# Opening of a two-layer fp32 trunk on one core: norm weights and activation table first, the norm factor ahead of the first column-wise blocks, and hidden-state transposes in two batches of four

## The chip, the cores and the metric

The kernel runs on one core of one Trainium2 chip. The metric is the device time of one execution in microseconds. The kernel before took 961.47 us (median of three runs, 961.28 to 961.77). Below, PE is TensorE's matrix multiply, PEld its weight load, DVE is VectorE, ACT is ScalarE, POOL is GpSimd, SP is SyncE. The last two only do small work here; SP issues nearly all loads.

## What is computed

The input is 256 rows of 1024 floats. Two layers follow each other; each is a half-step SwiGLU feed-forward block, a mixer and a second half-step feed-forward block, each behind an RMS norm, and a last norm ends the trunk:

```python
def rms_norm(x, g):
    y = x * rsqrt(mean(x * x, axis=-1, keepdims=True) + EPS)
    return y * g

def swiglu(x, w_gate, w_up, w_down):
    return (silu(x @ w_gate) * (x @ w_up)) @ w_down

for layer in range(2):
    h = h + 0.5 * swiglu(rms_norm(h, ffn1_norm[layer]), ...)      # 1024 -> 2816 -> 1024
    h = h + mixer(rms_norm(h, mix_norm[layer]), ...)
    h = h + 0.5 * swiglu(rms_norm(h, ffn2_norm[layer]), ...)
return rms_norm(h, final_norm)
```

The change touches only the first feed-forward block of layer 0 (`ffn(0, begin)`), that is, the opening of the kernel. The mixers (dilated attention with spatial gating in layer 0, block attention in layer 1) are not touched.

## The kernel before

**Precision.** Every fp32 product is made from three matmuls of a rounded format: an operand is split into a high part (`hi`, a rounded copy made on ACT) and a low part (`lo`, the rest, made on DVE by a subtraction), and the three are high by high, high by low and low by high. Weights are split as they arrive: `split_parts` (L79 on ACT, L80 on DVE), in two halves of 128x1024 for each 1 MB weight tile (tiles 0 and 1 in four quarters).

**The stream of weights.** `Stream` numbers the weight tiles in the order of their use. Each is 1 MB. Three raw buffers (`RAW = 3`) and four split buffers (`SPL = 4`) rotate: the load of tile j starts when tile j-3 has been split, and its split may start when PE has finished with tile j-4. `add` (L46) sets in how many DMAs a tile is loaded: four for tiles 0 and 1, two for tiles 2 and 3, one for all others. Tiles 0 and 1 are the gate weights of the first 512 hidden columns, 2 and 3 the up weights of the same columns; from tile 4 on gate and up tiles of 256 hidden columns alternate (4 and 5 for the third pair of hidden tiles, 6 and 7 for `k = 6`, 8 and 9 for `k = 8`, up to `k = 20`).

**The opening (`begin`, L431 to L539).** The first input is loaded already transposed (`xf`, eight tiles of 128x256, with `fetch`), multiplied by the norm weights `gT` and split into `xgh` and `xgl` (`part`, L470 and L471). The norm's factor for each row is not yet known. PE first runs 28 warm-up matmuls on zeros (`heat`, L429), then the first 512 gate columns and the first 512 up columns row-wise (`products`, L459, L462, L465) on `xgh`/`xgl` of tiles 0 to 3. Two blocks of 256 hidden columns follow column-wise (`colwise`, L352 to L354, 48 matmuls of 256 columns each): m = 0 with weight tile 4 and m = 1 with weight tile 5, both still on `xgh`/`xgl`.

Meanwhile `x` arrives by rows, its squares are summed, and POOL makes the factor `rstd` (L212). The factor is spread over all partitions: `dg` (L514) puts it on a diagonal, four plain fp32 matmul records of ones by `dg` (L515) put it in a PSUM bank `rb`, and two copies on ACT (L518) put it twice side by side in `rs`. With `rs` the transposed input is normed in place on DVE (L522, eight tiles) and split again into `xT["h"]` on ACT (L205) and `xT["l"]` on DVE (L206), in four pairs of tiles. All later column-wise blocks read `xT`. In the code before this whole chain stands inside m = 1, behind the split of weight tile 5 and ahead of the second column-wise block.

**After the opening.** For k = 6, 8, ... 20 two column-wise blocks (gate and up, 96 matmuls in all) give two tiles of the hidden state, `gated` (L554, L555) multiplies them and `keep` splits them into `hT`. The four hidden tiles of the first 512 columns were computed row-wise and must be transposed: `finish` leaves a function `turn` for each half of the rows in the list `todo`; a `turn` is four plain fp32 transposes on PE (L567) and a split (L205, L206). At k = 8 `turn_all` runs all that is in the list, which is both functions here. In the other three feed-forward blocks one `turn` runs before k = 4 and the other at k = 8. The block ends with `project`, the product with the down weights (L369, L370, L373).

**What sets the order.** The tile framework's planner writes each engine's order. `begin`, the two `finish` and one `keep` stand under `tc.manual_schedule()`: on each engine these keep the order in which they are written. Work from behind that block (the splits of weight tiles 6 to 9, for instance) may be put between them where the planner sees the engine free. Every engine runs its own list strictly in that order.

Of the kernel before, what the change touches and what calls it, by code (L numbers as in the profile page):

```python
# [10 lines left out]
F32 = mybir.dt.float32  # L11
F32R = mybir.dt.float32r
AF = mybir.ActivationFunctionType
ALU = mybir.AluOpType

S = 256
D = 1024
NT = S // 128
KD = D // 128
# [17 lines left out]
class Stream:  # L37
# [5 lines left out]
        self.loaded = self.split = self.done = self.next = 0  # L43

    def add(self, src, nk, w, shift=0, pieces=2):
        self.specs.append((src, nk, w, (4, 4, 2, 2)[len(self.specs)] if len(self.specs) < 4 else 1, shift, pieces))  # L46

    def load_one(self):
        for _ in self.load_parts():
# [68 lines left out]
def trunk(ctx: ExitStack, tc: tile.TileContext, a, out):  # L118
    nc = tc.nc
# [11 lines left out]
    def bank():  # L131
        return ps.tile([128, 512], F32, name="bank")
# [48 lines left out]
    gT = cp.tile([128, 6 * KD], F32, name="gT")  # L181
    xr = [cp.tile([128, D], F32, name=f"x{t}") for t in range(NT)]

    half_neg = cp.tile([128, 8], F32, name="half_neg")
    ident = cp.tile([128, 128], F32, name="ident")
# [7 lines left out]
    ones = cp.tile([128, 128], F32, name="ones")  # L193
# [10 lines left out]
    def split(hi, lo, src):  # L204
        nc.scalar.activation(hi, src, AF.Copy)  # L205
        nc.vector.tensor_sub(lo, src, hi.bitcast(F32))  # L206


    xT = {}
# [4 lines left out]
    pend, rstd = {}, {}  # L214
# [119 lines left out]
    def new_xT():  # L334
        xT["h"] = xp.tile([128, KD, NT, 128], F32R, name="xTh")
        xT["l"] = xp.tile([128, KD, NT, 128], F32R, name="xTl")
# [9 lines left out]
    def colwise(p, w, c, x=None):  # L346

        for k in range(KD):
            cs = slice(c * 128, (c + 1) * 128)
            h, l = w[0][:, k, cs], w[1][:, k, cs]  # L350
            xh, xl = [v[:, k] for v in (x or (xT["h"], xT["l"]))]
            nc.tensor.matmul(p, h, xh, start=k == 0, stop=False)  # L352
            nc.tensor.matmul(p, h, xl, start=False, stop=False)  # L353
            nc.tensor.matmul(p, l, xh, start=False, stop=k == KD - 1)  # L354
# [71 lines left out]
    def heat(n):  # L426

        for _ in range(n):
            nc.tensor.matmul(bank()[:, :128], warm, warm, start=True, stop=True)  # L429

    def begin(fp, pb):  # L431

        f = [fp.tile([128, KD, S], t, name=m) for t, m in ((F32, "xf"), (F32R, "xgh"), (F32R, "xgl"))]
        xf, xgh, xgl = f

        def fetch(k, n, engine):
            engine.dma_start(xf[:, k : k + n, :], a["xt"][:, k : k + n, :])

        fetch(0, 1, nc.scalar)
        nc.scalar.dma_start(gT, a["gt"])  # L440
        first = st.load_parts()
        next(first)
        fetch(1, 1, nc.sync)
        next(first)
        fetch(2, 2, nc.sync)
        for _ in first:
            pass
        fetch(4, 2, nc.sync)
        second = st.load_parts()
        next(second)  # L450
        next(second)
        fetch(6, 2, nc.sync)
        for _ in second:
            pass
        st.load_one()

        def products(m, w, k0, k):
            for t in range(NT):
                nc.tensor.matmul(pb[t, m], xgh[:, k0 + k, t * 128 : (t + 1) * 128], w[0][:, k, :],  # L459
                                 start=k0 + k == 0, stop=False)  # L460
            for t in range(NT):
                nc.tensor.matmul(pb[t, m], xgl[:, k0 + k, t * 128 : (t + 1) * 128], w[0][:, k, :],  # L462
                                 start=False, stop=False)
            for t in range(NT):
                nc.tensor.matmul(pb[t, m], xgh[:, k0 + k, t * 128 : (t + 1) * 128], w[1][:, k, :],  # L465
                                 start=False, stop=k0 + k == KD - 1)

        def part(k):
            g = gT[:, k : k + 1]
            nc.scalar.activation(xgh[:, k, :], xf[:, k, :], AF.Copy, scale=g)  # L470
            nc.vector.scalar_tensor_tensor(xgl[:, k, :], xf[:, k, :], g, xgh[:, k, :].bitcast(F32),  # L471
                                           op0=ALU.mult, op1=ALU.subtract)

        heat(HEAT)
        for m in range(2):
            for t in range(NT):
                pb[t, m] = bank()
        for i in range(2):
            parts = st.split_parts()
            for k in range(4):  # L480
                part(4 * i + k)
                next(parts)
            for _ in parts:
                pass
            st.load_one()
            if i == 0:
                for t in range(NT):
                    nc.sync.dma_start(xr[t], x[t * 128 : (t + 1) * 128, :])
            w = st.take_split()
            for k in range(4):  # L490
                products(0, w, 4 * i, k)
            st.free_split()
        for i in range(2):
            st.split_one()
            w = st.take_split()
            for k in range(4):
                products(1, w, 4 * i, k)
            st.free_split()
            st.load_one()
        for t in range(NT):  # L500
            pend[t].square(0)
            pend[t].square(1, nc.vector)
            pend[t].root()
        xg = [v.rearrange("p k (t c) -> p k t c", t=NT) for v in (xgh, xgl)]
        pair = []
        for m in range(2):
            st.split_one()
            w = st.take_split()
            p = bank()
            if m == 1:  # L510
                rb = bank()
                for t in range(NT):
                    dg = fp.tile([128, 128], F32, name="dg", bufs=2)
                    nc.vector.tensor_scalar(dg, ident, rstd[t], None, op0=ALU.mult)  # L514
                    nc.tensor.matmul(rb[:, t * 128 : (t + 1) * 128], ones, dg, start=True, stop=True)  # L515
                rs = fp.tile([128, 2, S], F32, name="rs")
                for j in range(2):
                    nc.scalar.copy(rs[:, j, :], rb[:, :S])  # L518
                new_xT()
                for k in range(0, KD, 2):  # L520
                    for i in range(k, k + 2):
                        nc.vector.scalar_tensor_tensor(xf[:, i, :], xf[:, i, :], gT[:, i : i + 1], rs[:, 0, :],  # L522
                                                       op0=ALU.mult, op1=ALU.mult)
                    xk = xf[:, k : k + 2, :].rearrange("p k (t c) -> p k t c", t=NT)
                    split(xT["h"][:, k : k + 2], xT["l"][:, k : k + 2], xk)
            for j in range(2):
                colwise(p[:, j * S : (j + 1) * S], w, j, xg)
            st.free_split()
            st.load_one()
            pair.append(p)  # L530
        rs = rs.rearrange("p j c -> p (j c)")
        g = fp.tile([128, 512], F32, name="hm", bufs=3)
        nc.vector.tensor_mul(g, pair[0], rs)
        sil = fp.tile([128, 512], F32, name="sil", bufs=2)
        nc.scalar.activation(sil, g, AF.Silu)
        nc.vector.tensor_mul(g, sil, pair[1])
        hm = fp.tile([128, 512], F32, name="hm", bufs=3)
        nc.vector.tensor_mul(hm, g, rs)
        return hm  # L539

    def ffn(phase, begin=None):
        with tc.tile_pool(name="fp", bufs=1) as fp:
# [5 lines left out]
            todo = []  # L548

            def gated(pg, pu, r=None):  # L550
                g = fp.tile([128, 512], F32, name="sil", bufs=2)
                hm = fp.tile([128, 512], F32, name="hm", bufs=3)
                if r is None:
                    nc.scalar.activation(g, pg, AF.Silu)  # L554
                    nc.vector.tensor_mul(hm, g, pu)  # L555
                else:
                    nc.scalar.activation(g, pg, AF.Silu, scale=r)
                    nc.vector.scalar_tensor_tensor(hm, pu, r, g, op0=ALU.mult, op1=ALU.mult)
                return hm
# [12 lines left out]
            def turn_all():  # L572
                for f in todo:
                    f()
                todo.clear()
# [14 lines left out]
            def keep(k, hm):  # L590
                split(hT[0][:, k : k + 2], hT[1][:, k : k + 2], hm.rearrange("p (k t c) -> p k t c", k=2, t=NT))
# [15 lines left out]
            for k in range(6 if begin else 4, FT, 2):  # L607
                ps2 = []
                for _ in range(2):
                    p = bank()  # L610
                    w = st.take()
                    for j in range(2):
                        colwise(p[:, j * S : (j + 1) * S], w, j)
                    st.free()
                    ps2.append(p)
                if k == 8:
                    turn_all()
                keep(k, gated(*ps2))
# [320 lines left out]
```

## Time and profile before

| what | value |
|---|---|
| time, median of three runs | 961.47 us |
| the profiled execution's own time | 961.31 us |
| its span | 959.6 us, granted TensorE clock 0.998 |
| PE busy | 945.0 us, 98% of the span |
| PEld busy | 863.5 us (90%) |
| DVE busy | 569.6 us (59%) |
| ACT busy | 512.3 us (53%) |
| POOL busy | 68.0 us (7%) |
| loaded and stored | 175.75 MB, 182 GB/s over the span |

A row of the timeline gives start, duration, engine, line, operation, output and inputs, and in brackets how long the engine sat idle before it and what ended that. A PE row's duration overlaps its neighbours', since matmuls are pipelined: what a matmul costs is the distance from one start to the next. A row of waits names who waited, on which line, for whom: microseconds in total, times, longest. Some PE records are missing from the trace, so PE work is measured between rows that are there and not by counting rows.

### The profile page before, as it was taken

To read this page: it belongs to the slowest core of one execution; us is meant where nothing else is said; L and a number is where in the kernel's file an instruction comes from. 1 tells how busy PE (TensorE), PEld (TensorE's weight loads), DVE (VectorE), ACT (ScalarE), POOL (GpSimd) and SP (SyncE) were. 2 spreads that over 40 slices of the span, in tenths; PEclk is the share of its full clock that TensorE was granted. 3 is DMA by queue.
4 is the path that set the end of the run, shared out by engine and by line. 5 is a ranking of instruction groups with operands and counts; after the bars stand their busy time and mean duration, and the time that the engine had idled before them with its cause. 6 is when DMAs were issued, how large, how long until landed. Compare 5 with 4: busy or idle time off the path is not lost.

```text
span 959.6 us, 15488 instructions
## 1 busy us (share of the span) xinstructions
PE 945.0 (98%) x6368; PEld 863.5 (90%) x6368; DVE 569.6 (59%) x831; ACT 512.3 (53%) x838; POOL 68.0 (7%) x105
## 2 busy tenths in 40 slices
PE   8999999999999999999999999999999999999997
PEld 7899998889978999988889999887999789999886
DVE  6775554468866655544555555346788666555443
ACT  6664443386867444443554444346787575444431
POOL 0000000010300000000000000000356300000000
PEclk9999999999999999999999999999999999999999
DMA  9865555647443866555466565564554438665521
GB/s 327 266 202 181 198 189 177 211 136 263 133 131 96 257 194 201 183 209 179 139 222 210 179 207 186 191 204 141 177 174 133 132 115 259 191 205 180 207 96 45
DMA packets 119431, 175.75 MB, mean 183 GB/s; under 512 B 3136, under 2 KB 92352, under 8 KB 119360
## 3 DMA queue, kind: packets, MB, share of 16 engines
q1 hardware_dynamic: 117536, 172.44, 54.8%
q10 hardware_dynamic: 1824, 2.32, 0.9%
q8 instruction: 50, 0.82, 0.3%
q14 instruction: 21, 0.17, 0.0%
HBM read 173.69 MB, written 1.05 MB: 182 GB/s over the span
## 4 chain that ended last, share of the span: by engine, by line
PE 90%; ACT 4%; DVE 3%; issue 1%; DMA 0%; POOL 0%; POOLq 0%; ACTq 0%; DVEq 0%
PE bank L353 16%; PE bank L354 16%; PE bank L352 15%; PE bank L373 9%; PE bank L369 9%; PE bank L370 9%; PE bank L344 4%; PE bank L342 4%; PE bank L343 4%; DVE wlo L80 2%; ACT whi L79 1%; PE bank L304 1%; ACT pr L667 1%; PE bank L459 1%; PE bank L462 1%
## 5 line engine op out<-in xcount | busy, mean ns | idle before, releaser
L80 DVE TENSOR_TENSOR wlo<-raw,whi 128x1024 fp32r<-128x1024 f32 (+1 forms) x336 | 385.7, 1186 | 228.3 <-ACT whi L79 227.5
L79 ACT ACTIVATE whi<-raw 128x1024 fp32r<-128x1024 f32 (+1 forms) x336 | 329.9, 1029 | 351.2 <-issue 217.7
L353 PE MATMUL bank<-xTl,whi 128*128 128x256 f32 x1344 | 372.5, 277 | 2.7 <-DVE xTl L206 2.7
L352 PE MATMUL bank<-xTh,whi 128*128 128x256 f32 x1344 | 373.6, 278 | 0.0
L354 PE MATMUL bank<-xTh,wlo 128*128 128x256 f32 x1344 | 372.1, 277 | 0.0
L353 PEld LDWEIGHTS bank<-xTl,whi 128*128 128x128 f32 x1344 | 252.6, 188 | 3.4 <-DVE xTl L206 3.3
L354 PEld LDWEIGHTS bank<-xTh,wlo 128*128 128x128 f32 x1344 | 253.1, 188 | 0.0
L352 PEld LDWEIGHTS bank<-xTh,whi 128*128 128x128 f32 x1344 | 252.1, 188 | 0.3 <-ACT xTh L205 0.2
L369 PE MATMUL bank<-whi,hTh 128*128 128x512 f32 x344 | 134.1, 390 | 0.0
L370 PE MATMUL bank<-wlo,hTh 128*128 128x512 f32 x344 | 133.9, 389 | 0.0
L373 PE MATMUL bank<-whi,hTl 128*128 128x512 f32 x344 | 110.6, 389 | 0.0
L373 PEld LDWEIGHTS bank<-whi,hTl 128*128 128x128 f32 x344 | 64.6, 188 | 13.5
L370 PEld LDWEIGHTS bank<-wlo,hTh 128*128 128x128 f32 x344 | 64.6, 188 | 13.2
L369 PEld LDWEIGHTS bank<-whi,hTh 128*128 128x128 f32 x344 | 64.6, 188 | 13.1
L555 DVE TENSOR_TENSOR hm<-sil,bank 128x512 f32<-128x512 f32 x41 | 28.2, 688 | 76.1 <-PE bank L354 71.3
L212 POOL TENSOR_TENSOR rstd<-ms,half_neg 128x1 f32<-128x1 f32 x14 | 12.7, 907 | 788.6 <-DVE ms L246 784.4
L342 PE MATMUL bank<-whi,xTh 128*128 128x512 f32 x160 | 63.1, 394 | 0.0
L344 PE MATMUL bank<-whi,xTl 128*128 128x512 f32 x160 | 62.5, 390 | 0.0
L343 PE MATMUL bank<-wlo,xTh 128*128 128x512 f32 x160 | 62.3, 390 | 0.0
L344 PEld LDWEIGHTS bank<-whi,xTl 128*128 128x128 f32 x160 | 30.0, 188 | 6.7 <-DVE xTl L316 0.4
L342 PEld LDWEIGHTS bank<-whi,xTh 128*128 128x128 f32 x160 | 30.0, 188 | 6.0
L343 PEld LDWEIGHTS bank<-wlo,xTh 128*128 128x128 f32 x160 | 30.1, 188 | 6.0
(133 smaller groups left out, 807.9 us busy)
## 6 DMA issues: line engine op xcount, KB each, us to landing
raw<-in_ffn_w_down SPq DMA_DIRECT2D x44, 1024.0 KB, 5.0
raw<-in_ffn_w_gate SPq DMA_DIRECT2D x42, 1024.0 KB, 5.5
raw<-in_ffn_w_up SPq DMA_DIRECT2D x42, 1024.0 KB, 5.4
raw<-in_c_w_in SPq DMA_DIRECT2D x12, 1024.0 KB, 5.2
raw<-in_ab_w_in SPq DMA_DIRECT2D x10, 1024.0 KB, 5.4
raw<-in_ab_w_out SPq DMA_DIRECT2D x4, 1024.0 KB, 5.0
raw<-in_c_w_out SPq DMA_DIRECT2D x4, 1024.0 KB, 4.9
raw<-in_ffn_w_gate SPq DMA_DIRECT2D x8, 256.0 KB, 5.5
```

The costliest lines, as they stand in the source:

```text
L79: nc.scalar.activation(hi[:, a : a + h], raw[:, a : a + h], AF.Copy)
L80: nc.vector.tensor_sub(lo[:, a : a + h], raw[:, a : a + h], hi[:, a : a + h].bitcast(F32))
L342: nc.tensor.matmul(p, xh, w[0][:, k, :], start=k0 + k == 0, stop=False)
L343: nc.tensor.matmul(p, xh, w[1][:, k, :], start=False, stop=False)
L344: nc.tensor.matmul(p, xl, w[0][:, k, :], start=False, stop=k0 + k == KD - 1)
L352: nc.tensor.matmul(p, h, xh, start=k == 0, stop=False)
L353: nc.tensor.matmul(p, h, xl, start=False, stop=False)
L354: nc.tensor.matmul(p, l, xh, start=False, stop=k == KD - 1)
L369: nc.tensor.matmul(banks[t, h], sh, w[0][:, kw, cs], start=first, stop=False)
L370: nc.tensor.matmul(banks[t, h], sh, w[1][:, kw, cs], start=False, stop=False)
L373: nc.tensor.matmul(banks[t, h], sl, w[0][:, kw, cs], start=False, stop=last)
L555: nc.vector.tensor_mul(hm, g, pu)
```

## The change

Four edits, all in the opening:

1. The load of the norm weights `gT` is now the first DMA on ACT; the first tile of `xf` moves to SP, ahead of the first weight piece, and the second tile of `xf` moves from SP to ACT. Behind these two DMAs ACT gets a small copy of `half_neg` to a new tile `begun`, so that ACT's function table is loaded there.
2. Weight tiles 4 and 5 are loaded in two DMAs each.
3. The spread of the factor (`dg`, the fp32 matmuls) moves ahead of the split of weight tile 4. The copies to `rs` follow the split of tile 4. The norm and split of `xT` is cut in two: tiles 0 to 3 between the splits of weight tiles 4 and 5 (inside m = 0), tiles 4 to 7 behind the split of weight tile 5 (inside m = 1).
4. At k = 6 of this feed-forward block the first `turn` is taken off the list and run, so that k = 8 runs only the second.

```diff
     def add(self, src, nk, w, shift=0, pieces=2):
-        self.specs.append((src, nk, w, (4, 4, 2, 2)[len(self.specs)] if len(self.specs) < 4 else 1, shift, pieces))
+        self.specs.append((src, nk, w, 4 if len(self.specs) < 2 else 2 if len(self.specs) < 6 else 1, shift, pieces))
...
-        fetch(0, 1, nc.scalar)
         nc.scalar.dma_start(gT, a["gt"])
+        fetch(0, 1, nc.sync)
         first = st.load_parts()
         next(first)
-        fetch(1, 1, nc.sync)
+        fetch(1, 1, nc.scalar)
+        nc.scalar.activation(fp.tile([128, 8], F32, name="begun"), half_neg, AF.Copy)
         next(first)
         fetch(2, 2, nc.sync)
...
+        rb = bank()
+        for t in range(NT):
+            dg = fp.tile([128, 128], F32, name="dg", bufs=2)
+            nc.vector.tensor_scalar(dg, ident, rstd[t], None, op0=ALU.mult)
+            nc.tensor.matmul(rb[:, t * 128 : (t + 1) * 128], ones, dg, start=True, stop=True)
+        rs = fp.tile([128, 2, S], F32, name="rs")
+        new_xT()
+
+        def normed(k0):
+            for k in range(k0, k0 + 4, 2):
+                for i in range(k, k + 2):
+                    nc.vector.scalar_tensor_tensor(xf[:, i, :], xf[:, i, :], gT[:, i : i + 1], rs[:, 0, :],
+                                                   op0=ALU.mult, op1=ALU.mult)
+                xk = xf[:, k : k + 2, :].rearrange("p k (t c) -> p k t c", t=NT)
+                split(xT["h"][:, k : k + 2], xT["l"][:, k : k + 2], xk)
+
         pair = []
         for m in range(2):
             st.split_one()
+            if m == 0:
+                for j in range(2):
+                    nc.scalar.copy(rs[:, j, :], rb[:, :S])
+            normed(4 * m)
             w = st.take_split()
             p = bank()
-            if m == 1:
-                rb = bank()
...
             for j in range(2):
                 colwise(p[:, j * S : (j + 1) * S], w, j, xg)
...
                     ps2.append(p)
+                if k == 6 and begin:
+                    todo.pop(0)()
                 if k == 8:
                     turn_all()
                 keep(k, gated(*ps2))
```

The lines left out behind `if m == 1:` are the same spread, copies, norm and split in their old place.

More of the change, by code (lines that the diff above doesn't have):

```diff
@@ L507, in begin @@
             st.split_one()
+            if m == 0:
+                for j in range(2):
+                    nc.scalar.copy(rs[:, j, :], rb[:, :S])
+            normed(4 * m)
             w = st.take_split()
             p = bank()
-            if m == 1:
-                rb = bank()
[L512 to L525, printed above, removed]
             for j in range(2):
```

## The prediction

> **What bounds the kernel now.** I read the page's head first, then the list of waits of PE, then the timeline where those waits lie.
>
> ```profile
> span 959.6 us, 15488 instructions
> PE 945.0 (98%) x6368; PEld 863.5 (90%) x6368; DVE 569.6 (59%) x831; ACT 512.3 (53%) x838; POOL 68.0 (7%) x105
> PE bank L353 <- DVE xTl L206: 2.7, 3, 1.7
> PE bank L459 <- ACT whi L79: 1.5, 1, 1.5
> ```
>
> PE is the bound from end to end. A change can only help by taking away a wait of PE or by letting PE run its matmuls faster. The two longest waits of the whole list lie in the opening that the change rewrites: 1.5 us before the first real matmul and 2.7 us on `xTl`. What PE gains there reaches the end, since PE is busy 98% of the time behind it.
>
> The first wait in the timeline (start, duration, engine, line), and under it three answers on single DMAs with the time from issue to landing:
>
> ```profile
> 0.79 0.39 SPq L60 DMA_DIRECT2D raw<-in_ffn_w_gate  x1
> 0.79 0.41 ACTq L437 DMA_DIRECT2D xf<-in_xt  x1
> 1.10 4.86 PE L429 MATMUL bank<-warm 128*128 128x128 f32 x28 [1.10 <-DVE warm L191]
> 1.23 0.45 ACTq L440 DMA_DIRECT2D gT<-in_gt  x1
> 5.12 1.28 ACT L470 ACT_TABLE_LOAD   x1 [5.12 <-DMA gT<-in_gt]
> 6.41 0.51 ACT L470 ACTIVATE xgh<-xf,gT 128x256 fp32r<-128x256 f32 x1
> 6.82 0.61 ACT L79 ACTIVATE whi<-raw 128x512 fp32r<-128x512 f32 x1
> 7.49 0.74 PE L459 MATMUL bank<-whi,xgh 128*128 128x512 f32 x2 [1.53 <-ACT whi L79]
> ...
> raw<-in_ffn_w_gate SPq DMA_DIRECT2D x1, 256.0 KB, 3.7
> xf<-in_xt ACTq DMA_DIRECT2D x1, 128.0 KB, 3.8
> gT<-in_gt ACTq DMA_DIRECT2D x1, 24.0 KB, 3.8
> ```
>
> `gT`, issued second on ACT, lands at 1.23 + 3.8 = 5.03, when the first weight piece (0.79 + 3.7 = 4.49) and the first `xf` tile (0.79 + 3.8 = 4.59) are already there. Only then does ACT load its table for 1.28 us, and the first real matmul starts at 7.49, 1.53 us after the warm-up ended at 5.96.
>
> The second wait:
>
> ```profile
> 31.27 2.01 ACT L79 ACTIVATE whi<-raw 128x1024 fp32r<-128x1024 f32 x2 [0.91 <-DMA raw<-in_ffn_w_gate]
> 35.08 0.61 PE L515 MATMUL bank<-dg,ones 128*128 128x128 f32 x4
> 35.44 0.37 PE L352 MATMUL bank<-xgh,whi 128*128 128x256 f32 x1
> 35.72 0.65 ACT L518 COPY rs<-bank 128x256 f32<-128x256 f32 x2 [2.44 <-PE bank L515]
> 36.13 0.88 DVE L522 SCALAR_TENSOR_TENSOR xf<-xf,gT,rs 128x256 f32<-128x256 f32 x2 [1.41 <-ACT rs L518]
> 37.22 0.63 ACT L205 ACTIVATE xTh<-xf 128x512 fp32r<-128x512 f32 x1
> 37.36 1.23 DVE L80 TENSOR_TENSOR wlo<-raw,whi 128x1024 fp32r<-128x1024 f32 x1 [0.36 <-ACT whi L79]
> 48.36 0.69 DVE L206 TENSOR_TENSOR xTl<-xf,xTh 128x512 fp32r<-128x512 f32 x1
> 40.98 0.28 PE L352 MATMUL bank<-xTh,whi 128*128 128x256 f32 x1
> 66.67 1.04 PE L567 MATMUL bank<-ident,hm 128*128 128x128 f32 x8
> ```
>
> The factor is spread at 35.08, after the first column-wise block. Norm and split then last from 36.13 to 49.05, because splits of later weight tiles (`wlo`) are put between their steps on DVE, while PE needs the first `xT` tile at 40.98 already.
>
> A third loss stands in no list of waits. These are the DVE rows of `gated`, each released by the last matmul of a pair of blocks (96 matmuls), first in this feed-forward block and then in the next one, with the fp32 batches around them:
>
> ```profile
> 66.93 0.69 DVE L555 TENSOR_TENSOR hm<-sil,bank 128x512 f32<-128x512 f32 x1 [2.16 <-issue]
> 79.12 0.69 DVE L555 TENSOR_TENSOR hm<-sil,bank 128x512 f32<-128x512 f32 x1 [2.34 <-PE bank L354]
> 135.66 0.69 DVE L555 TENSOR_TENSOR hm<-sil,bank 128x512 f32<-128x512 f32 x1 [2.34 <-PE bank L354]
> ...
> 314.27 0.60 PE L567 MATMUL bank<-ident,hm 128*128 128x128 f32 x4
> 347.37 0.60 PE L567 MATMUL bank<-ident,hm 128*128 128x128 f32 x4
> 347.64 0.69 DVE L555 TENSOR_TENSOR hm<-sil,bank 128x512 f32<-128x512 f32 x1 [2.12 <-PE bank L354]
> 358.97 0.69 DVE L555 TENSOR_TENSOR hm<-sil,bank 128x512 f32<-128x512 f32 x1 [2.12 <-PE bank L354]
> 402.50 0.69 DVE L555 TENSOR_TENSOR hm<-sil,bank 128x512 f32<-128x512 f32 x1 [2.11 <-PE bank L354]
> ```
>
> In the next block a pair takes (402.50 - 358.97) / 4 = 10.88 us, 113 ns a matmul. In this one it takes (135.66 - 79.12) / 5 = 11.31 us, 118 ns, with the same shapes. The step comes at a batch of plain fp32 work: before the eight transposes at 66.67 the matmuls follow each other at 113 ns, behind them at 118; before the four L515 records at 35.08 they stand at (35.08 - 29.42) / 48 = 118 ns, behind them at (40.98 - 35.44) / 48 = 115 ns with their restart. A later place shows both sizes again:
>
> ```profile
> 29.42 0.28 PE L352 MATMUL bank<-xgh,whi 128*128 128x256 f32 x1
> ...
> 204.51 1.03 PE L304 MATMUL bank<-ident,xn 128*128 128x128 f32 x8
> 219.02 0.28 PE L352 MATMUL bank<-xTh,whi 128*128 128x256 f32 x1
> 221.73 0.28 PE L354 MATMUL bank<-xTh,wlo 128*128 128x256 f32 x1
> 221.84 0.60 PE L731 MATMUL bank<-ident,wsp 128*128 128x128 f32 x4
> 222.99 0.28 PE L352 MATMUL bank<-xTh,whi 128*128 128x256 f32 x1
> 223.90 0.28 PE L354 MATMUL bank<-xTh,wlo 128*128 128x256 f32 x1
> ```
>
> After a batch of eight: (221.73 - 219.02) / 23 = 118 ns. After a batch of four: (223.90 - 222.99) / 8 = 114 ns. I read this as: a batch of eight leaves PE in a slow pace, a batch of four in a fast one. Why, the trace doesn't tell.
>
> **The change part by part. First, the start.** The table load moves behind ACT's two DMA issues, to about 1.7, and hides under the wait for data; the copy that triggers it lies there too and costs nothing as long as the landings come after 3.3 (1.7 + 1.28, and a small copy). `gT` issued at 0.79 should land near 4.6, `xf` on SP the same; the first weight piece, now issued at 1.23 behind 128 KB of `xf`, at 4.9 to 5.4. ACT then needs 0.41 (6.41 to 6.82) from `xgh` to the weight split, and PE follows 0.67 after the latter's start (6.82 to 7.49): first matmul at 5.6 to 6.1. But the warm-up, unchanged, ends at 5.96. I take 6.05, a gain of 1.4; the bounds are 1.53 (the whole wait) and 0.9 (weight piece at 5.9). Behind the first piece PE takes (29.42 - 7.49) / 16 = 1.37 us a piece while DMA order and bytes stay nearly the same, so I count no further wait; a late second or third piece is what the lower bound is for.
>
> [...]
>
> **Second, two more DMA issues** (tiles 4 and 5 in halves), 0.4 us each on SP by the rows above, cover: SP only waits for buffers there. Their gain is that ACT can split half a tile while the rest arrives. PE needs neither earlier than now, so nothing; if SP's cover were gone, up to 0.8 us later loads.
>
> **Third, the factor.** The same `dg`, matmuls, copies and norm steps run, so nothing is added; what counts is what they now stand in front of. The L515 records move from 35.08 to the place of 29.42, which is 28.0 after the first gain. Copies start 0.64 later, the norm 0.41 after that: 29.0 instead of 36.13. One pair of tiles without anything between takes 0.88 (DVE) + 0.63 (ACT) + 0.69 (DVE), about 2.15 with overlaps, so two pairs end near 33.3. Only now may tile 5 be split, on ACT and DVE in written order: its first `wlo` half is ready near 34.8. PE starts m = 0 at 28.4, ends it at the fast pace (48 x 113 ns = 5.44) at 33.9, and its third matmul of m = 1 wants that half at 34.1. So 0.7 us of a new wait at the least. If the planner puts halves of tile 6's split between, as it does now with later tiles, each adds up to 1.2 us. Behind it, tiles 4 to 7 of the norm end near 40.3, when PE at k = 6 wants them from 41.5 on: no wait, or up to 1.7 us if four halves of splits are put in (4 x 1.2, less 1.3 of DVE's idle time between the steps, less the slack of 1.8 from 40.3 to 42.1, where PE takes the last pair).
>
> Of the old wait, the whole loss is more than the 2.7 listed: from 40.98 to 66.67 two pairs ran, 2 x 10.88 = 21.77 us of work in 25.69, so 3.9 us with restarts. I leave 2.0 us of new waits: between 0.7 and 3.9, nearer to the first, since the old chain started 7 us later. Gain 1.9, bounds 0 and 3.2. The 48 matmuls of m = 0 run at the fast pace behind L515: 48 x 5 ns, 0.2 more, bounds 0 and 0.2.
>
> **Fourth, transposes.** The records stay eight: a batch of eight costs 79.12 - 66.93 - 11.31 = 0.88 us, a batch of four 358.97 - 347.64 - 10.88 = 0.45; twice that is 0.90, a loss of 0.02. `turn` at k = 6 needs `hm` of the first rows, which DVE makes behind the last `xTl`, now at 48.36 and by the steps above 8 us earlier, while PE gets there two blocks after 40, near 51. If each batch of four leaves the fast pace, the pairs k = 10 to 20 gain 6 x 0.43 = 2.6 us. Bounds 0 and 2.6: nothing in the rows makes a batch of four worse than eight.
>
> **The sum.** 1.4 + 1.9 + 0.2 + 2.6 = 6.1 (the 0.02 is lost in rounding), so 961.31 - 6.1 = 955.2 for a profiled execution. The median of the runs lies 0.16 above that execution: 955.4. With the terms at their bounds, 7.5 and 0.9, the span of outcomes is 954.0 to 960.6.
>
> **The rivals.**
>
> *The pace isn't set by the batch* but by something that happens to change at 66.67. For it: no row names a cause, and this happens once in this block. Against it: three changes of pace quoted above fall on such a batch. Time: 955.4 + 2.6 = 958.0. [...]
>
> *The wait on `xT` only moves* to tile 5's split. ACT runs strictly in order, and tile 6 lands at about 31.2 (row 31.27). If the planner places its split ahead of `xTh`, ACT stands until then. Its first half ends at 32.2 on ACT and 33.5 on DVE, the first `xTl` at 34.1, the norm's next two steps at 35.0, the second half of tile 6 and the second `xTl` at 36.7, the first half of tile 5 at 37.9: PE waits 3.8 us in m = 1 instead of 3.9 later. For it: the planner did put tile 6 ahead of the copies before (31.27 against 35.72). Against: there PE was 4 us from giving the factor when tile 6 landed; now it gives it 3 us before. Time: 955.4 + 1.9 = 957.3.
>
> *The start doesn't move*, because the first weight piece behind `xf` on one queue lands after 6: 955.4 + 1.4 = 956.8.
>
> *Slower: the later blocks lose the fast pace.* All work behind the opening is planned anew. Each of the other three feed-forward blocks runs nine pairs (k = 4 to 20); if its two batches came together as one of eight, they would go at 11.31 instead of 10.88, 3.9 us a block. One block leaves a gain, two end at 963.1, three at 967.0: it decides from the third. For it: that is what this block does today. Against: their code and data are unchanged, and their batches stand a whole pair and more apart (314.27 and 347.37).
>
> **How the numbers follow.** Forecast 0.63 (953.4 to 957.0), pace rival 0.13, moved wait 0.14, start 0.05, slower 0.05. A measurement of this kernel tells 0.2% (1.9 us) from no change. The forecast, the start and most of the two middle rivals stay faster than that; 0.04 of the moved wait goes to cases where the pace fails as well (near 960), 0.03 of the pace rival to cases where the start fails with it, and both are no change. So 0.63 + 0.05 + 0.10 + 0.10 = 0.88 faster, 0.07 the same, 0.05 slower. The range of 953.4 to 958.9 holds the forecast and the first rivals' own times; its low end lies 0.6 below the bounds' 954.0, should even the 0.7 us of new wait be hidden.
>
> **What would show it.** The first L459 row at 6.0 to 6.1, with the warm-up's end as its only limit. L515 near 28, and one wait of PE on `wlo` L80 in m = 1 of 0.7 to 2 us instead of the three on `xTl`. L567 in two records of four, 11 us apart, and L555 rows 10.88 us apart behind the second. It would be wrong if L555 stays at 11.31, if PE waits 4 us in m = 1, or if the blocks behind 200 us take longer than now.

## The result, and the profile after

The changed kernel takes 954.73 us (median of five runs, 953.54 to 957.22); the kernel before took 961.28 us beside it (959.57 to 961.77). The medians lie 6.5 us apart. The ratio is 0.9937, with a 95% interval of 0.992 to 0.9954, which makes it 6.1 us (4.4 to 7.7). The profiled execution of after happens to be the longest of the five, 957.22 us, and that matters below. Its page's head and the first part of its list of waits (microseconds in total, times, longest):

```profile
span 955.5 us, 15493 instructions
PE 944.4 (99%) x6368; PEld 863.8 (90%) x6368; DVE 569.5 (60%) x831; ACT 512.4 (54%) x839; POOL 68.1 (7%) x105
PE bank L304 <- DVE xn L284: 1.2, 1, 1.2
PE bank L429 <- DVE warm L191: 1.1, 1, 1.1
PE bank L354 <- DVE wlo L80: 0.8, 1, 0.8
```

The 1.5 us ahead of the first real matmul and the 2.7 us on `xTl` are gone. What is new is a wait of 0.8 us on a low half of weight tile 5 (`wlo`). The timeline of the start (lines are shifted by the edit: L460 is the first product, L471 makes `xgh`):

```profile
0.79 0.41 ACTq L439 DMA_DIRECT2D gT<-in_gt  x1
1.10 5.13 PE L429 MATMUL bank<-warm 128*128 128x128 f32 x28 [1.10 <-DVE warm L191]
1.71 1.28 ACT L444 ACT_TABLE_LOAD   x1 [1.71 <-PEq L928]
3.01 0.21 ACT L444 ACTIVATE begun<-half_neg 128x8 f32<-128x8 f32 x1
4.07 0.51 ACT L471 ACTIVATE xgh<-xf,gT 128x256 fp32r<-128x256 f32 x1 [0.85 <-DMA gT<-in_gt]
5.39 0.63 ACT L79 ACTIVATE whi<-raw 128x512 fp32r<-128x512 f32 x1 [0.81 <-DMA raw<-in_ffn_w_gate]
6.07 0.73 PE L460 MATMUL bank<-whi,xgh 128*128 128x512 f32 x2
```

The table is loaded at 1.71, long before `xgh` can start at 4.07, on the landing of `gT`. PE starts at 6.07 instead of 7.49, and no wait is listed: the split of the first weight piece ends at 6.02 (5.39 + 0.63), just as the warm-up runs out (its last matmul ends at 1.10 + 5.13 = 6.23, overlapped by the first real one). The same timeline further on (L510 spreads the factor, L517 norms, L572 transposes h):

```profile
27.99 0.60 PE L510 MATMUL bank<-dg,ones 128*128 128x128 f32 x4
28.63 0.65 ACT L527 COPY rs<-bank 128x256 f32<-128x256 f32 x2 [2.97 <-PE bank L510]
29.04 0.88 DVE L517 SCALAR_TENSOR_TENSOR xf<-xf,gT,rs 128x256 f32<-128x256 f32 x2 [2.12 <-ACT rs L527]
32.80 0.69 DVE L206 TENSOR_TENSOR xTl<-xf,xTh 128x512 fp32r<-128x512 f32 x1 [0.70 <-ACT xTh L205]
33.75 2.36 DVE L80 TENSOR_TENSOR wlo<-raw,whi 128x1024 fp32r<-128x1024 f32 x2 [0.26 <-ACT whi L79]
35.03 0.38 PE L354 MATMUL bank<-xgh,wlo 128*128 128x256 f32 x1 [0.76 <-DVE wlo L80]
40.55 0.28 PE L352 MATMUL bank<-xTh,whi 128*128 128x256 f32 x1
41.63 0.68 DVE L206 TENSOR_TENSOR xTl<-xf,xTh 128x512 fp32r<-128x512 f32 x1
51.86 0.60 PE L572 MATMUL bank<-ident,hm 128*128 128x128 f32 x4
63.22 0.60 PE L572 MATMUL bank<-ident,hm 128*128 128x128 f32 x4
```

The norm starts at 29.04 instead of 36.13; when PE takes the first `xT` tile at 40.55 only the last pair is still open, and PE doesn't wait for it. The transposes come in two batches of four. Behind the second, though, the pairs of blocks in this execution are as slow as before. The rows of `gated`, first in this block (ends of the pairs k = 10 and k = 20), then in the next feed-forward block (k = 10 and k = 18):

```profile
75.23 0.69 DVE L560 TENSOR_TENSOR hm<-sil,bank 128x512 f32<-128x512 f32 x1 [2.34 <-PE bank L354]
131.77 0.69 DVE L560 TENSOR_TENSOR hm<-sil,bank 128x512 f32<-128x512 f32 x1 [2.34 <-PE bank L354]
...
355.03 0.69 DVE L560 TENSOR_TENSOR hm<-sil,bank 128x512 f32<-128x512 f32 x1 [2.12 <-PE bank L354]
398.55 0.69 DVE L560 TENSOR_TENSOR hm<-sil,bank 128x512 f32<-128x512 f32 x1 [2.11 <-PE bank L354]
```

(131.77 - 75.23) / 5 = 11.31 us a pair here, (398.55 - 355.03) / 4 = 10.88 there. So this one execution shows the gain of the start and of the factor, and none of the transposes.

### The profile page after: what moved, and what is told of

Same layout as the page of the kernel before. It is cut to its first block, busy times and chain, and to the rows that moved or that the text cites. A ratio compares the mean times of both kernels' runs of the same rounds, so it can differ in the third digit from the quotient of the medians.

```text
span 955.5 us, 15493 instructions
## 1 busy us (share of the span) xinstructions
PE 944.4 (99%) x6368; PEld 863.8 (90%) x6368; DVE 569.5 (60%) x831; ACT 512.4 (54%) x839; POOL 68.1 (7%) x105
## 4 chain that ended last, share of the span: by engine, by line
PE 91%; ACT 4%; DVE 3%; issue 1%; POOL 0%; POOLq 0%; DVEq 0%; ACTq 0%
PE bank L354 16%; PE bank L352 16%; PE bank L353 16%; PE bank L373 9%; PE bank L369 9%; PE bank L370 9%; PE bank L344 4%; PE bank L342 4%; PE bank L343 4%; DVE wlo L80 2%; ACT whi L79 1%; PE bank L304 1%; ACT pr L674 1%; PE bank L460 1%; PE bank L463 1%
## 5 line engine op out<-in xcount | busy, mean ns | idle before, releaser
L352 PE MATMUL bank<-xTh,whi 128*128 128x256 f32 x1344 | 374.1, 278 | 0.0
L352 PEld LDWEIGHTS bank<-xTh,whi 128*128 128x128 f32 x1344 | 252.3, 188 | 0.1
```

## The experiments

All ratios are against the kernel before on the same chip.

| kernel | median us (range) | before beside it | ratio (95%) |
|---|---|---|---|
| again: the changed kernel | 954.46 (953.78 to 955.3) | 962.27 | 0.992 (0.9903 to 0.9936) |
| fours_only: edit 4 alone | 959.69 (958.5 to 961.8) | 962.27 | 0.998 (0.9966 to 0.9993) |
| no_fours: the change without edit 4 | 957.57 (956.34 to 957.75) | 962.27 | 0.995 (0.9933 to 0.9966) |
| start_only: edit 1 alone | 959.3 (957.02 to 960.24) | 962.27 | 0.9969 (0.9958 to 0.9979) |
| factor_only: edit 3 alone | 958.27 (956.41 to 959.64) | 961.24 | 0.9967 (0.9954 to 0.998) |
| earlier5: norm cut 2 + 6 tiles | 954.62 (954.18 to 954.89) | 961.24 | 0.9927 (0.9915 to 0.9939) |
| sizes, sizes2: extra transposes | 974.08, 974.55 (one run each) | 961.24 | |
| before_again: the kernel before | 961.89 (961.28 to 964.8) | 961.99 | 1.0002 (0.9992 to 1.0013) |
| heat10: shorter warm-up | 954.46 (954.24 to 954.73) | 961.99 | 0.9923 (0.9906 to 0.9941) |
| interleave: tile 5 between norm steps | 955.15 (954.38 to 957.11) | 961.99 | 0.9934 (0.9917 to 0.9951) |
| best: both of these | 954.37 (954.19 to 954.53) | 961.99 | 0.9922 (0.9905 to 0.9939) |

**The changed kernel once more** (no edit), since the profile of after lacked a gain that its own median seemed to hold.

> The changed kernel once more, to see its pace in another execution. If the size of a batch sets the pace and the slow stretch of the first profile (pairs of 11.31 us behind 63 us) was an exception, this profile shows pairs of 10.88 us there and a time near 954.7. If the pace is drawn anew in each execution, the profile's time and its pairs go together: near 957.2 with 11.31, near 954.7 with 10.88, and the timed runs spread over both. If the kernel always runs slow there, pairs are 11.31 again and the 2.5 us between the first profile and the median come from somewhere else.

Its profiled execution took 954.79 us. Its timeline at the places of after's:

```profile
5.77 0.71 PE L460 MATMUL bank<-whi,xgh 128*128 128x512 f32 x2
28.17 0.60 PE L510 MATMUL bank<-dg,ones 128*128 128x128 f32 x4
63.38 0.60 PE L572 MATMUL bank<-ident,hm 128*128 128x128 f32 x4
74.99 0.69 DVE L560 TENSOR_TENSOR hm<-sil,bank 128x512 f32<-128x512 f32 x1 [2.12 <-PE bank L354]
129.12 0.39 PE L369 MATMUL bank<-whi,hTh 128*128 128x512 f32 x1
129.39 0.69 DVE L560 TENSOR_TENSOR hm<-sil,bank 128x512 f32<-128x512 f32 x1 [2.12 <-PE bank L354]
```

Here a pair behind 63.38 takes (129.39 - 74.99) / 5 = 10.88 us. Same code, same batch of four, another pace than in the profile of after: `project` starts at 129.12 there and at 131.50 in after's profile. Of the eleven timed runs of this code one took 957.22 and the others 953.54 to 955.3. The 2.4 us that the one lost are the transposes' gain. That the gain came in the rest is shown by a trace for the profiled run of `again`, and by their times alone for the other nine.

**Edit 4 alone.**

```diff
+                if k == 6 and begin:
+                    todo.pop(0)()
                 if k == 8:
                     turn_all()
```

> The kernel before with only the transposes taken apart (one batch of four at k = 6, one at k = 8). If the size of the batch sets the pace: 2.6 us faster, 958.7, pairs k = 10 to 20 at 10.88 us. If the pace has nothing to do with it: 961.3, pairs at 11.31. If it is drawn anew each time: something between, with a spread of 2.6 us.

```profile
67.09 0.60 PE L567 MATMUL bank<-ident,hm 128*128 128x128 f32 x4
78.70 0.69 DVE L555 TENSOR_TENSOR hm<-sil,bank 128x512 f32<-128x512 f32 x1 [2.12 <-PE bank L354]
133.10 0.69 DVE L555 TENSOR_TENSOR hm<-sil,bank 128x512 f32<-128x512 f32 x1 [2.12 <-PE bank L354]
```

(133.10 - 78.70) / 5 = 10.88: the edit alone gives the fast pace. The medians differ by 962.27 - 959.69 = 2.6 us; the ratio makes it 1.9 (0.7 to 3.3). The twelve runs fall in two groups, eight at 958.5 to 960.1 and four at 961.4 to 961.8, about the worth of the edit apart; only one run, of the first group, was profiled, and the kernel before spread from 959.37 to 964.2 beside it, so it isn't shown that the second group lost the pace.

**The change without edit 4.**

```diff
-                if k == 6 and begin:
-                    todo.pop(0)()
```

> The changed kernel with both transposes at k = 8 as before, so one batch of eight. Size theory: pairs at 11.31 us in every execution, time about 957.2, with little spread. Draw theory: a median like that of the changed kernel, 954.7, and the same spread.

```profile
63.19 1.04 PE L572 MATMUL bank<-ident,hm 128*128 128x128 f32 x8
75.64 0.69 DVE L560 TENSOR_TENSOR hm<-sil,bank 128x512 f32<-128x512 f32 x1 [2.34 <-PE bank L354]
132.18 0.69 DVE L560 TENSOR_TENSOR hm<-sil,bank 128x512 f32<-128x512 f32 x1 [2.34 <-PE bank L354]
```

One batch of eight again, and (132.18 - 75.64) / 5 = 11.31. It lies 957.57 - 954.46 = 3.1 us above the whole change. So edit 4 is worth about as much on top of the others as alone, and about what the pace accounts for. Over all profiles of this case the pace here was slow behind a batch of eight in five of five, and fast behind the second batch of four in eight of nine (the ninth is the profile of after). The rival that edit 4 is worth nothing falls. Edit 4 changes the size of the batch and also the place of the first one, though, and this run doesn't tell the two apart.

**Edit 1 alone** (DMA order and the early copy, as in the diff of the change):

```diff
-        fetch(0, 1, nc.scalar)
         nc.scalar.dma_start(gT, a["gt"])
+        fetch(0, 1, nc.sync)
...
+        nc.scalar.activation(fp.tile([128, 8], F32, name="begun"), half_neg, AF.Copy)
```

> The kernel before with only the start changed (norm weights first, first input tile on SP, small copy for the table). The first real matmul at 6.05 instead of 7.49. If the gain of 1.4 us is carried to the end: 959.9. If the earlier start runs into the wait on xTl (PE there earlier by 1.4 while DVE's chain hangs on the same spread matmuls, so it moves too): still 1.4. If weight tiles arrive too late for it, PE waits at weight tile 4 or 5 and less than 1 us is left: 960.5 or more.

```profile
6.39 0.71 PE L460 MATMUL bank<-whi,xgh 128*128 128x512 f32 x2
...
PE bank L353 <- DVE xTl L206: 1.8, 2, 1.2
```

In the profile PE starts 7.49 - 6.39 = 1.10 us earlier and ends 1.55 us earlier (953.01 to 951.46). The wait on `xTl` shrinks from 2.7 to 1.8, but behind it the matmuls go at 118 ns, which takes half of that back. The runs give 962.27 - 959.3 = 3.0, twice that, with an interval of 2.0 to 4.0. Of the difference 962.27 - 961.31 = 1.0 lies in the kernel before, which took longer on this chip than in its profiled execution, and 959.82 - 959.3 = 0.5 in this kernel's own spread; I can't point to either in a trace.

**Edit 3 alone** (spread, copies and the two calls of `normed` as in the change, loads and transposes as before; in part):

```diff
...
+            if m == 0:
+                for j in range(2):
+                    nc.scalar.copy(rs[:, j, :], rb[:, :S])
+            normed(4 * m)
             w = st.take_split()
...
```

> The kernel before with only the factor's spread, norm and split of the transposed input moved ahead (old start, old loads of weight tiles 4 and 5, one batch of eight transposes). My steps give 1.9 us from the wait on xTl and 0.2 from the first column-wise block's pace: 2.1 less than the kernel before on the same chip. If the new wait in m = 1 is 0.8 us as in the changed kernel's profile and no other takes its place: 3.1 less. If the old wait only moves to weight tile 5: no difference.

```profile
36.74 0.39 PE L354 MATMUL bank<-xgh,wlo 128*128 128x256 f32 x1 [0.76 <-DVE wlo L80]
```

The same new wait as in the change, and PE has no other from the first product to the transposes; tile 5 comes in one DMA here, so edit 2 has no part in it. The ratio of 0.9967 is 3.2 us (1.9 to 4.4). The profiled execution is one of the two longest of the six, 959.37: behind the wait PE is slow for 238 matmuls, until the transposes, which costs it 238 x 4.5 ns = 1.1 us. By the ratios the three edits alone add up to 0.20 + 0.31 + 0.33 = 0.84%, the whole change to 0.63% in its first measurement and 0.80% in again; the intervals are too wide to show whether anything is lost between them.

**Taking the new wait away, first way**: tiles 0 and 1 of the norm ahead of tile 5's split, the other six behind.

```diff
...
-            normed(4 * m)
+            normed(*((0, 2), (2, KD))[m])
```

> The changed kernel with only one pair of normed tiles, not two, ahead of weight tile 5's split, so that this split comes about 2.2 us earlier on DVE. If the remaining wait of PE in m = 1 (0.76 us, on that split's low half) and the slow pace that follows it (144 matmuls at 118 instead of 113 ns until the first batch of transposes, 0.65 us) hang together: both go, 1.4 us less than the changed kernel, 953.1. If the pace doesn't depend on the wait: 0.8 less. If the later norm pairs then come too late for k = 6: PE waits on xTl again and little is gained.

```profile
PE bank L352 <- ACT xTh L205: 0.7, 1, 0.7
```

The wait on `wlo` is gone, m = 1 runs at the fast pace, and k = 6 now waits 0.7 for `xTh`: 954.62 us, a ratio of 0.9927 against 0.992. The loss moves with the order of DVE's work. DVE has nearly no slack there: in after it idles 0.70 + 0.70 + 0.26 = 1.7 us from 29.04 to 42.31.

**Which batches set the pace?** Transposes of `ident` that nobody reads are put behind pairs k = 10 to 18 of all four feed-forward blocks, in numbers from 1 to 16; added work, so only the pace behind them counts.

```diff
...
+                if 10 <= k <= 18:
+                    for i in range(SIZES[phase][k // 2 - 5]):
+                        if i % 4 == 0:
+                            spare = bank()
+                        nc.tensor.transpose(spare[:, i % 4 * 128 : (i % 4 + 1) * 128], ident, ident)
```

> The changed kernel with extra fp32 transposes of the identity into a bank that nothing reads, one batch behind each pair k = 10, 12, 14, 16, 18: in the first feed-forward block 8, 1, 8, 2, 8 of them, in the second 8, 3, 8, 4, 8, in the third 5, 6, 7, 4, 6, in the last 8, 4, 12, 4, 16. They cost about 0.11 us each, 14 us in all, and the sum of batches says nothing; what is read is the pace of the pair behind each. Size theory: 118 ns behind every 8, 113 behind every 4, with a border between that 5, 6 and 7 show. Draw theory: both paces behind both sizes without order. Total-length theory (the pace is a matter of how long PE was off the stream): 5 to 16 all slow, 1 to 4 all fast.

> The same with the lists in other blocks (first block 5, 6, 7, 4, 6; second 8, 4, 12, 4, 16; third 8, 1, 8, 2, 8; last 8, 3, 8, 4, 8). If the size decides, each size has the pace that it had in the other run; if the block or the weight buffers in use decide, the paces stay with the places; if it is a draw, they agree with neither.

From the last feed-forward block of sizes2, batches of 8, 4 and 8, with the row of `gated` behind each:

```profile
870.72 1.03 PE L630 MATMUL bank<-ident 128*128 128x128 f32 x8
870.99 0.69 DVE L561 TENSOR_TENSOR hm<-sil,bank 128x512 f32<-128x512 f32 x1 [2.34 <-PE bank L355]
882.90 0.60 PE L630 MATMUL bank<-ident 128*128 128x128 f32 x4
883.17 0.69 DVE L561 TENSOR_TENSOR hm<-sil,bank 128x512 f32<-128x512 f32 x1 [2.34 <-PE bank L355]
894.65 1.03 PE L630 MATMUL bank<-ident 128*128 128x128 f32 x8
894.92 0.69 DVE L561 TENSOR_TENSOR hm<-sil,bank 128x512 f32<-128x512 f32 x1 [2.34 <-PE bank L355]
906.69 0.69 DVE L561 TENSOR_TENSOR hm<-sil,bank 128x512 f32<-128x512 f32 x1 [2.12 <-PE bank L355]
```

The intervals are 12.18, 11.75 and 11.77. Less the batch itself (0.88, 0.45, 0.88) that is 11.30, 11.30 and 10.89: slow behind eight, slow behind four, fast behind eight. So the size alone doesn't decide. Over the profiled executions of all fourteen runs in this case (before and after included), measured from start to start of the 256-column matmuls behind a batch (and, in the last two rows, straight behind row-wise matmuls of 512 columns):

| what stands ahead | fast pace behind it |
|---|---|
| h's transposes, four at a time | 101 of 102 (the miss is after's, at 63.22) |
| the factor's spread, four | 14 of 14 |
| spatial weights' transposes, four | 14 of 14 |
| h's transposes, eight at once | 0 of 5 |
| attention probabilities' transposes, three | 78 of 84 |
| extra: 1, 2, 3 | 2 of 2, 1 of 2, 0 of 2 |
| extra: 4 | 2 of 8 |
| extra: 5, 6, 7 | 2 of 2, 3 of 4, 0 of 2 |
| extra: 8 | 3 of 14 |
| extra: 12, 16 | 2 of 2, 2 of 2 |
| row-wise products of the opening, no batch | 0 of 4 |
| row-wise products of the mixers (xn's eight transposes lie 7 to 15 us ahead of the stretch) | 0 of 28 |

The kernel's own fours nearly always leave PE fast, its own eights never, and between them no rule of the number holds: an extra four is mostly slow, twelve and sixteen were fast. The total-length theory of `sizes` falls with these. Between `sizes` and `sizes2` the lists change blocks: at the same place the two runs agree in 11 of 20 batches, at the same position of the same list in 17 of 20. So the pace went with the list more than with the block, and yet within the list 8, 3, 8, 4, 8 the first two eights were slow and the last fast, in both runs. By the code a batch of more than four also writes to more than one `bank()`, and no run keeps that apart. Within a stretch of column-wise blocks between two interruptions the pace held, but for the first one to four matmuls; it changes at a batch, at a wait or behind row-wise products. A wait can go either way: behind the `wlo` wait of m = 1 it was slow in after, again, factor_only and sizes2, and fast in no_fours, heat10 and sizes. One place gives mostly the same pace from execution to execution, but not always: the six slow cases of the attention's transposes all lie at one place, where eight other executions were fast. The sum of sizes fits: 130 extra transposes at 0.11 us and 11 pairs turned slow at 0.43 are 19.0 us, measured 974.08 - 954.46 = 19.6 (against the changed kernel on another chip). What decides the pace stays open.

**The kernel before once more** (no edit), for its own spread of starts.

> The kernel before, unchanged, timed against itself. It shows how far two sets of runs of one kernel stand apart, and gives a second look at its start and pace. If the paces are drawn anew in each execution, single runs spread over some 2.5 to 4 us and the ratio's interval holds 1. If the order on the engines fixes them, this profile has the same paces at the same places as the first one: 118 ns up to the spread of the factor, 113 up to the batch of eight, 118 behind it, and a first real matmul at 7.5.

The start in its timeline, and then one row of the view by windows from before (the first) and from this run (the second). The columns are window, length, and for PE and PEld the busy time with the number of instructions under way in the window (x); DVE, ACT and POOL, the granted clock, the DMA share and GB/s follow:

```profile
1.10 6.04 PE L429 MATMUL bank<-warm 128*128 128x128 f32 x28 [1.10 <-DVE warm L191]
7.74 0.74 PE L459 MATMUL bank<-whi,xgh 128*128 128x512 f32 x2 [0.59 <-ACT whi L79]
```

```profile
4.60:5.40 0.80, 0.80 (x10) 0.80 (x9) 0.00 (x0) 0.28 (x1) 0.00 (x0) 1.00 0.77 236
```

```profile
4.60:5.40 0.80, 0.80 (x6) 0.80 (x5) 0.00 (x0) 0.03 (x1) 0.00 (x0) 1.00 0.89 279
```

The time is that of the kernel before, but the warm-up lasts 6.04 us where before's lasted 4.86. In the same 0.8 us ten warm-up matmuls are under way in before and six in this run. They go at 213 ns each and, from some matmul on, at 111; the step comes 2.94 us after the first warm-up matmul in before, 3.57 in after, 5.50 here, and in no_fours not within the 28 at all. The paces of the column-wise blocks lie at the same places as in before, but for one stretch behind three of the attention's transposes. The twelve runs still spread over 3.5 us, and one profile doesn't show why.

**A shorter warm-up**, 20 matmuls for 28.

```diff
-HEAT = 14
+HEAT = 10
```

> The changed kernel with a warm-up of 20 matmuls instead of 28. In the profiles of the changed start the warm-up ended the wait before the first real matmul more often than the data did: the first weight split was ready near 5.6 to 6.2 in all of them, the first real matmul came between 5.8 and 7.1, since the warm-up took 4.9 to 6.3 us. If the warm-up is the limit: the first real matmul at 5.6 to 6.2 in this profile, and 0 to 1.2, on the mean about 0.5 us less than the changed kernel (954.0). If the array is not yet fast after 20 matmuls: the first real matmuls run at about twice their spacing for a while, and the gain is lost.

```profile
1.10 4.17 PE L429 MATMUL bank<-warm 128*128 128x128 f32 x20 [1.10 <-DVE warm L191]
5.95 0.63 ACT L79 ACTIVATE whi<-raw 128x512 fp32r<-128x512 f32 x1 [1.81 <-DMA raw<-in_ffn_w_gate]
6.63 0.73 PE L460 MATMUL bank<-whi,xgh 128*128 128x512 f32 x2 [1.36 <-ACT whi L79]
```

The warm-up ends at 5.27, and now PE waits 1.36 us for the first weight piece, whose split starts on its landing, at 5.95 in this execution (4.88 to 5.51 in the profiles that start the same way with 28). Nothing is gained: 954.46, as the changed kernel. The two limits of the start lie that close together.

**Taking the new wait away, second way**: the halves of tile 5's split between the norm's first steps.

```diff
...
+                five = st.split_parts()
+                normed(0, lambda k: next(five))
...
```

> The changed kernel with the two halves of weight tile 5's split put between the steps of the first norm half: the first half behind the first pair of tiles, the second half in DVE's wait for the second pair's high part. The wait of 0.76 us in m = 1 should go, and no step of the norm comes later than now, so PE shouldn't wait on xTh or xTl at k = 6 as it did where only one pair stood ahead. If so: 0.8 us less than the changed kernel, 953.7, and 0.65 more if the slow pace behind the wait goes with it (953.1). If the total of DVE's work up to k = 6 is the limit: the wait turns up there again and the time stays at 954.5.

```profile
PE bank L353 <- DVE xTl L206: 0.3, 1, 0.3
PE bank L352 <- ACT xTh L205: 0.2, 1, 0.2
```

The `wlo` wait of 0.8 is replaced by 0.5 at k = 6. 955.15 us; not to be told from the changed kernel.

**Both together** (`HEAT = 10` and the interleaved split).

> Both together, the warm-up of 20 and the interleaved split. If the two gains add: 952.6 to 953.2. If the earlier start only meets DVE's chain earlier: like interleave alone, 953.1 to 953.7.

954.37 us, ratio 0.9922 against 0.992 for the change itself. Its list of waits has 0.9 for the first weight piece and 0.4 at k = 6. No version beats the changed kernel measurably.

## Why the prediction was right, and where it wasn't

Predicted were 955.4 us (953.4 to 958.9); measured are 954.73. The terms against three profiled executions: before (961.31), again (954.79, near the median) and after (957.22). Landmarks are the end of the products (before's first L352 row at 29.42, the spread at 28.17 and 27.99), the end of k = 8 ahead of the transposes (66.67; 63.38 and 63.22, each less 0.45 for the first batch, which is already done there), and the start of `project` (135.39, 129.12, 131.50).

| term | predicted | again | after |
|---|---|---|---|
| start | 1.4 | 29.42 - 28.17 = 1.25 | 1.43 |
| factor chain and pace of m = 0 | 1.9 + 0.2 | 37.25 - 34.76 = 2.49 | 2.47 |
| transposes | 2.6 | 68.72 - 66.19 = 2.53 | 0 |
| up to `project` | 6.1 | 6.27 | 3.89 |
| last matmul | | 953.01 - 946.60 = 6.41 | 953.01 - 949.02 = 3.99 |

**The start: right in its mechanism, wrong in what limits it.** The step "the warm-up, unchanged, ends at 5.96" named the right limit and took it for a constant. With 28 matmuls the warm-up lasted 4.80 to 6.29 us in the traces, because its step from 213 to 111 ns comes at different times, and the new start mostly follows its end: first matmuls lay from 5.66 to 7.10. In seven of the eight profiles with the new start and 28 warm-up matmuls they began 0.03 to 0.07 us behind the start of the last warm-up matmul; in after the split of the first weight piece ended last, 0.05 us before PE began. Before, the table load hid this spread: its starts lie at 7.48 to 7.78. On the mean, the products end at 29.54 in the four profiles with the old start and at 28.41 in the eight with the new start and 28 warm-up matmuls: a gain of 1.1, and 0.5 to 1.5 in a single execution. The 1.4 was a good execution's value. The lower bound of 0.9 came from a late weight piece; such a piece came once, in heat10 (first matmul at 6.63), but the lowest gains came from a long warm-up. The steps lie from 2.9 to beyond 5.9 us behind the first warm-up matmul, a spread of 3 us. What sets their time is not shown; the view by windows has a granted clock of 1.00 at both rates and doesn't tell them apart.

**The table load** is hidden, as said: in after it ends at 1.71 + 1.28 = 2.99, the small copy begins at 3.01, and `xgh`, which waits for `gT`, at 4.07.

**The factor: the steps came nearly to the tenth, but the allowance for waits was mis-sized.** The spread was put near 28 (27.99), the norm at 29.0 (29.04), tile 5's first low half near 34.8, with 0.7 us of wait "at the least"; the wait is 0.76, up to 35.03. The step that failed is "I leave 2.0 us of new waits": the wait in m = 1 stayed at its least, and k = 6 waits for nothing. That is 3.9 - 0.8 = 3.1 instead of 1.9. Splits of later tiles did come between the norm's steps, as the prediction feared (on DVE 2.35 us at 36.82 and 1.22 at 40.49), and the norm ended at 42.31 and not near 40.3. PE began with the last pair's low half 0.48 us later, and 0.20 to 0.22 later in the profiles where m = 1 ran fast, so that no wait came was close. What came instead was something that the prediction didn't have: behind the wait in m = 1 PE fell into the slow pace for the 142 matmuls up to the transposes, 142 x 4.5 ns = 0.6 us. 3.1 + 0.2 - 0.6 = 2.7, against 2.49 measured. Two errors of opposite sign left the term 0.4 us too small.

**The transposes: the size was right, its reason only half.** 2.6 predicted, 2.53 in again, 2.6 and 3.1 by the medians with edit 4 alone and without it. But the step "a batch of eight leaves PE in a slow pace, a batch of four in a fast one" isn't a rule: extra fours were mostly slow, twelve and sixteen fast, and after's own second batch of four left PE slow once. It described h's own batches: the fours left PE fast 101 times of 102, the eights slow five times of five. One of the examples that it was read from doesn't show it: between the eight transposes at 204.51 and the slow stretch at 219.02 lie 13.7 us of row-wise matmuls, and behind row-wise products alone, as at 29.42, the pace is slow as well. That the size came out with a reason that isn't a rule is luck: edit 4 hit a place that behaves like the others of its kind. The first rival (the pace isn't set by the batch, 958.0) was wrong, by their times, in what it foretold for ten of the eleven runs, and 957.22, near its 958.0, is what the kernel takes when the pace fails. As to the cause it was nearer: something besides the size of the batch decides.

**The other rivals.** The wait did not move whole to tile 5 (0.8 of 3.9). The start moved. The later blocks kept 10.88 us a pair. The halved loads of tiles 4 and 5 (edit 2) were predicted to bring nothing; no run tried them alone, and in factor_only, without them, the wait in m = 1 is the same 0.76.

## What to carry to other kernels

When a wait is taken away at the start of an engine's work, ask which limit is next and whether it is a constant: here a table load that took 1.28 us in every trace gave way to a warm-up whose length differs by 1.5 us from one execution to the next. Measure PE's work in start-to-start distance, not in busy time: one of the two largest terms of this change, 2.5 us, stood in no list of waits. And where a rule is read from two or three places of one trace, its size may be used for those places, while its reason needs an experiment that changes only that.

## What the runs showed of the hardware

At one shape and a granted clock of 1.00 (the view by windows of before, after and again, 68 to 76 us of each) the matmuls of 256 columns had two paces, 113 and 118 ns from start to start. The pace changed at an interruption (a batch of fp32 matmuls, a wait or a run of row-wise products) and, but for the first one to four matmuls, held until the next one. Straight behind row-wise products of 512 columns it was slow in 32 of 32 stretches. Which one came elsewhere was mostly, but not always, the same at one place of one program (fast behind the attention's batches of three in 78 of 84, the six slow ones all at one place where eight other executions were fast); the size of the batch alone, from 1 to 16, didn't decide it, and its cause is open. The warm-up's step from 213 to 111 ns came anywhere from 2.9 us after its first matmul to after its 28th, 5.9 us on.
